# A hybrid decoder step on one core: linear attention's queries and keys decayed in place, and a planner that iterates with backward priorities

## The chip, the cores and the metric

The kernel runs on one core of one Trainium2 chip. The metric is the device time of one execution in microseconds (us), from the first to the last instruction and what lies around them. Five instruction streams run side by side: PE (TensorE, matmuls), DVE (VectorE), ACT (ScalarE), POOL (GpSimd) and SP (SyncE, which here issues all DMAs). Each works its own stream strictly in order.

## The reference

One decoder layer with two mixers side by side. For 2048 prompt rows and 64 sample rows (8 requests of 8 tokens):

```python
h = rmsnorm(x, norm_w)
q, k, v, qb, kb, vb, g_lr, gate_a, gate_b = split(h @ w_in)
o_a = attend(rope(rmsnorm(q)), rope(rmsnorm(k)), v)      # three dilated windows, 8 heads x 64
log_a = log_sigmoid(g_lr @ w_gate_up + b_gate) / 16       # one decay per token, head and key dim
o_b, s_fin = gla_chunked(qb / 8, kb, vb, log_a, s0)       # gated linear attention, 4 heads
y = x + concat(o_a * silu(gate_a), rmsnorm(o_b) * silu(gate_b)) @ w_out
```

Linear attention, for a chunk with `b = cumsum(log_a)`: the score of query t and key s ≤ t is the sum over key dims of `q[t] * k[s] * exp(b[t] - b[s])`; the output adds `q * exp(b)` times the state before the chunk; the new state is `exp(b_last) * state + (k * exp(b_last - b))^T v`. The outputs also hold the new keys and values and the states, for prompt and samples.

## The kernel before

All is float32 in and out. Projections and attention products run as pairs of f16 parts, linear attention in f32. The work has four stages, with the PE's projections woven through all of them:

1. Projections of v, q and k (`acc_v`, `acc_q`, `acc_k`; helper line L1614), row tiles of 128.
2. Dilated attention: scores `s` (L894) into PSUM, mask and maximum on DVE (L902), Exp on ACT (`p`, L905), transposes `t` on PE (L912), the split into f16 parts `pt` (ACT L874/L878, DVE L875, POOL L879), values `O` (L927). Beside it run the sample queries' scores against the key cache, called dots here: 104 loads of cached keys and 64 of queries, 128 products `pr` on POOL (L1469), each followed by a sum `sck` on DVE (L1470). The projections `acc_qkb`, then `acc_g` and `acc_vb`, fill PE.
3. Linear attention (`gla_core`, `gla_prompt`): the sample rows, then eight pieces `e` of 256 tokens, two chunks of 128 each. Seven levels B = 1, 2, 4 ... 64 build the scores within a chunk: at level B the queries of every second block of B tokens meet the keys of the block before. Each level needs scaled keys `ks` (L702), scaled queries laid out for two heads `qbd` (L706), matmuls `sc` (L730, L715) and a masked copy of the result (L736). The rest of `g`, `vb` and then `gb` projections fill PE; `so_gb` is the gate's SiLU on DVE (L1163, L1171), and `gw` its product on POOL (L1255).
4. Output: `combine` mixes the three attention branches and linear attention (`mix`), the mix is split and transposed (`mt`, `tm`), and `Y` (L1985) multiplies by `w_out`, whose f16 parts `w_o` are made by ACT L1144 and DVE L1145. The samples' attention over values (`OS`) fills in.

What sets the order: the program is traced, and then the class `Plan` writes one order for each of the five streams by hand. `depend` finds what must precede what, `price` gives each instruction a busy time and a latency, `rank` the longest path from each instruction to the end, `order` runs a list schedule with those ranks as priorities, and `fix` pins the result. So any change of a price or priority can move instructions anywhere in the program, within the dependences and the room in the buffers.

## Time and profile before

| | us |
|---|---|
| median of 3 runs (lowest to highest) | 1388.49 (1387.33 to 1389.8) |
| the profiled execution | 1387.66 |
| its span, first to last instruction | 1385.1 |
| PE busy | 1244.2 (90%) |
| DVE busy | 1008.1 (73%) |
| ACT busy | 844.7 (61%) |
| POOL busy | 639.5 (46%) |
| mean granted PE clock | 0.970 |

A row of the timeline gives the start, the duration, the engine, the source line, the operation, output<-inputs and a count; in square brackets stands how long the engine sat idle before and what ended that. A row of a table by stretches gives the stretch, its length, the busy time and instruction count of each engine it names (PE, PEld, DVE, ACT, POOL in this order), then the granted PE clock, the DMA engines' mean busy share and GB/s. In the groups, `x56 | 51.3, 921 | 11.9` reads: 56 instructions, 51.3 us busy, 921 ns each, 11.9 us idle before them. An f32 matmul is counted twice in the PE's rows (two records each).

### The profile page before, as it was taken

Reading aid. Unit: us, or ns where it says so; the run is one execution under the profiler, and the core shown is the slowest. Engines: PE = TensorE matmul, PEld = TensorE weight load, DVE = VectorE, ACT = ScalarE, POOL = GpSimd, SP = SyncE. Lnnn points to the kernel's source line nnn. Section 1 sums busy time; section 2 is a strip of 40 time slices with the busy share of each in tenths; the row PEclk is TensorE's granted clock in tenths of the full one; section 3 lists DMA queues with packets and bytes.
Section 4 is the critical chain, followed back from the end, with each engine's and each line's share of the span. In section 5 each row is a group of like instructions: output and inputs, shape, how many; then the busy total and the mean of one; then the engine's idle time right before and its main releaser. Section 6 shows DMA issues by size and latency. Waiting matters only on the chain.

```text
span 1385.1 us, 26375 instructions
## 1 busy us (share of the span) xinstructions
PE 1244.2 (90%) x8942; PEld 739.4 (53%) x8942; DVE 1008.1 (73%) x2459; ACT 844.7 (61%) x2259; POOL 639.5 (46%) x564
## 2 busy tenths in 40 slices
PE   5999988987889789998899999999989839999998
PEld 2444455555456556655667656665555415445443
DVE  6897787888889978767665338778889775566632
ACT  6465588786678869776778347787768541222220
POOL 0155447787677555543212546645574332233310
PEclk9999999998999999999999999999999969999999
DMA  8579747968986797899765534325334389999822
GB/s 298 179 194 268 206 132 202 226 199 213 207 288 178 170 308 242 248 249 280 187 181 154 144 102 110 109 84 179 103 100 145 104 309 344 343 380 345 323 79 70
DMA packets 236121, 283.25 MB, mean 205 GB/s; under 512 B 116353, under 2 KB 147154, under 8 KB 232914
## 3 DMA queue, kind: packets, MB, share of 16 engines
q1 hardware_dynamic: 235986, 281.57, 67.9%
q8 instruction: 70, 1.15, 0.4%
q14 instruction: 65, 0.53, 0.1%
HBM read 183.19 MB, written 75.24 MB: 187 GB/s over the span
## 4 chain that ended last, share of the span: by engine, by line
PE 36%; DVE 8%; ACT 7%; DMA 6%; issue 3%; POOL 1%; SPq 1%; DVEq 0%; ACTq 0%; POOLq 0%
PE Y L1985 10%; PE acc_vb L1614 4%; PE acc_g L1614 4%; PE acc_gb L1614 4%; DMA qb<-q_d 2%; PE OS L2234 1%; PE sc_e L730 1%; ACT p L905 1%; PE t L912 1%; PE O L1791 1%; PE acc_qkb L1614 1%; DMA o_d<-o 1%; DVE qbd L706 1%; PE O L1785 1%; PE O L927 1%
## 5 line engine op out<-in xcount | busy, mean ns | idle before, releaser
L1614 PEld LDWEIGHTS <-hr 128*128 128x128 f16 x1824 | 175.1, 99 | 125.0 <-issue 29.7
L1469 POOL TENSOR_TENSOR pr<-k,qb 128x512 f32<-128x512 f32 x128 | 176.9, 1382 | 133.4 <-DVE sck L1470 62.7
L905 ACT ACTIVATE p<-p,o 128x256 f32<-128x256 f32 (+1 forms) x384 | 172.7, 453 | 53.5 <-DVE o L902 43.7
L1614 PEld LDWEIGHTS <-hl 128*128 128x128 f16 x1248 | 119.7, 98 | 128.2 <-issue 18.7
L1985 PE MATMUL Y<-w_o,mh 128*128 128x512 f16 x768 | 181.1, 381 | 3.6 <-DVE xr L1992 1.7
L927 PE MATMUL O<-v,pt 128*128 128x128 f16 x1200 | 145.9, 224 | 8.6 <-POOL pt L879 3.5
L879 POOL TENSOR_TENSOR pt<-p,pt 128x512 f16<-128x512 f32 (+1 forms) x80 | 93.0, 1163 | 125.6 <-ACT pt L878 94.7
L912 PE MATMUL t<-ident,p 128*128 128x128 f32 x600 | 132.2, 294 | 16.3 <-ACT p L905 10.4
L1614 PE MATMUL acc_g<-w_g,hr 128*128 128x272 f16 (+1 forms) x768 | 130.6, 276 | 3.3 <-ACT vbs L1263 2.0
L1614 PE MATMUL acc_vb<-w_vb,hr 128*128 128x512 f16 x384 | 122.1, 384 | 1.6 <-DVE so_g L1163 1.5
L927 PEld LDWEIGHTS <-pt 128*128 128x128 f16 x1200 | 100.2, 101 | 43.3 <-POOL pt L879 7.2
L1470 DVE TENSOR_REDUCE sck<-pr 128x8 f32<-128x512 f32 x128 | 87.3, 682 | 48.9 <-POOL pr L1469 48.2
L1614 PE MATMUL acc_v<-w_v,hl 128*128 128x512 f16 x384 | 120.2, 384 | 2.0 <-DMA hl<-ht 1.0
L1614 PE MATMUL acc_k<-w_k,hl 128*128 128x512 f16 x384 | 114.8, 379 | 4.5 <-DVE vp L1276 2.9
L1614 PE MATMUL acc_q<-w_q,hl 128*128 128x512 f16 x384 | 116.2, 379 | 2.8 <-ACT zs_q L1189 2.4
L1985 PEld LDWEIGHTS <-mh 128*128 128x128 f16 x768 | 71.2, 98 | 84.5 <-issue 7.5
L894 PE MATMUL s<-kk,qq 128*128 128x256 f16 (+1 forms) x512 | 84.8, 270 | 29.4 <-DVE o L902 21.7
L912 PEld LDWEIGHTS t<-ident,p 128*128 128x128 f32 x600 | 79.3, 147 | 50.1 <-ACT p L905 28.0
L1614 PE MATMUL acc_gb<-w_gb,hr 128*128 128x512 f16 x384 | 95.7, 399 | 7.8 <-DVE so_gb L1163 7.8
L902 DVE CUSTOM_DVE_ANT_0 p<-s,m3w,scl_s 128x128 f32<-128x128 f32 (+1 forms) x256 | 87.8, 396 | 19.8 <-DMA o_d<-o 8.9
L2033 POOL TENSOR_TENSOR tc<-oc,w 128x512 f32<-128x512 f32 x32 | 42.8, 1354 | 118.7 <-DVE w L2025 67.9
L1614 PE MATMUL acc_qkb<-w_qkb,hr 128*128 128x512 f16 x288 | 85.1, 379 | 0.0
(534 smaller groups left out, 2723.1 us busy)
## 6 DMA issues: line engine op xcount, KB each, us to landing
k<-in_cache_k_win SPq DMA_DIRECT2D x104, 256.0 KB
sv_b<-in_cache_v_win SPq DMA_DIRECT2D x24, 1024.0 KB
hr<-h_d SPq DMA_DIRECT2D x44, 512.0 KB
qb<-q_d SPq DMA_DIRECT2D x64, 256.0 KB
oc<-o_d SPq DMA_DIRECT2D x48, 264.0 KB
o_d<-o SPq DMA_DIRECT2D x64, 132.0 KB
x<-in_x_prompt SPq DMA_DIRECT2D x16, 512.0 KB
h_d<-hl SPq DMA_DIRECT2D x16, 512.0 KB
```

The source lines that it names most:

```text
L706: DVE.tensor_tensor(qbd[:, :, :n].rearrange("p i (m B) -> p i m B", B=B), qv[:, :, 1, :].unsqueeze(1).to_broadcast([P, 2, M, B]), ev[:, 1: ...
L879: POOL.tensor_tensor(l, f, h, ALU.subtract)
L894: PE.matmul(s_ps[:, i * w : (i + 1) * w], q, k, start=(n == 0), stop=(n == len(prods) - 1),)
L902: DVE.tensor_tensor_reduce(s[:, sl], s_ps[:, sl], mask, neg, BIG, ALU.add, ALU.min, nmf(i))
L905: ACT.activation(s[:, sl], s[:, sl], AF.Exp, bias=nmf(i), scale=-1.0, accum_out=denf(i))
L912: PE.transpose(p_ps[:, i * P : (i + 1) * P], t["s"][:, i * P : (i + 1) * P], ident[:])
L927: PE.matmul(o_, t["pt"][:, c, (i * nb + b) * P : (i * nb + b + 1) * P], vf(i, b), start=(n == 0), stop=(n == 2 * nb - 1),)
L1469: POOL.tensor_tensor(pr[:], kt, qt, ALU.mult)
L1470: DVE.tensor_reduce(out, pr[:].rearrange("p (u k d) -> p u k d", u=2, k=4), AX.X, ALU.add)
L1614: PE.matmul(z, a_[:, k, :], w[:, p_, k, cols], start=(k == 0 and i == 0), stop=(k == KT - 1 and i == 2),)
L1985: PE.matmul(Y[:], a_[:, k, :], w_[:, part, k, :512], start=(i == 0), stop=(i == len(prods) - 1),)
L2033: eng.tensor_tensor(t_[:], oc[:, g, :, 0:64], w[:, g].unsqueeze(2).to_broadcast([P, NH, HD]), ALU.mult,)
```

## The change

**Linear attention.** Before, `b` is the running sum of the log decays (a scan on DVE, L673), and every level takes differences of `b` to the block's edge (two POOL subtractions `D`, L690 and L691), three Exps on ACT (`E`, L695) and two DVE multiplications into fresh buffers `ks` and `qbd`; all seven levels depend only on `b`. Now the decays themselves are used, `d = exp(log_a)`. Queries are multiplied by `d` once. At each level, two ACT copies spread the current queries into `qbd`, and the matmuls read the keys where they lie. After that, `decay()` multiplies in place: keys of even blocks by the odd neighbour's product (POOL), queries of odd blocks by the even neighbour's product (DVE), and a short DVE product pairs the block products up for the next level. After the last level the tile holds the queries decayed from the chunk's start and the keys decayed to its end, so the separate `qe` and `kd` work is gone. Each level now changes the tile that the next one reads. The buffer `kq` has three copies instead of two, `qbd` three, and `E`, `ks`, `D`, `b`, `eb` are gone. The matmuls are the same in number and shape.

```diff
@@ Plan.order
-                if not line or wide[0][0] <= line[0][0] + (bias if mode else -bias):
+                while recent and recent[0][0] < t - self.window:
+                    active -= recent.popleft()[1]
+                keep = mode and active > self.least * self.window
+                if not line or wide[0][0] <= line[0][0] + (bias if keep else -bias):
...
+                if int(s // self.window) > turn:
+                    half = work < 0.4 * self.window or int(s // self.window) > turn + 1
+                    turn, work = int(s // self.window), 0.0
...
+                own = self.busy[n] * (2 if half else 1)
@@ Plan, new
+    def settle(self, rounds, land, traffic, cross, bias, others=4):
...
+        others = [true.other(k) for k in range(others)]
+        self.lands = {n: x + land for n, x in self.lands.items()}
...
+        for _ in range(rounds):
+            out = self.order(prio, bias)[1]
+            prio = [-x for x in self.backward(self.start)]
+            end = sum(o.replay(out) for o in others)
+            if best is None or end < best[0]:
+                best = end, out
+        return best[1]
@@ gla_core
-        b = gt.tile([P, 2, n], F32, name=f"b_{tagp}", tag="bg", bufs=2)
-        for p in range(2):
-            DVE.tensor_tensor_scan(
-                b[:, p, :], scan_m[:, :n], la[:, p, :], 0.0, ALU.mult, ALU.add
-            )
-        eb = gt.tile([P, 2, n], F32, name=f"eb_{tagp}", tag="eb", bufs=2)
-        ACT.activation(eb[:], b[:], AF.Exp, scale=1.0 / 16.0)
+        ACT.activation(d[:], laf, AF.Exp, scale=1.0 / 16.0)
+        q, k = (f.rearrange("p a c -> p (a c)") for f in (qT, kT))
+        DVE.tensor_tensor(q, q, d[:], ALU.mult)
...
-            POOL.tensor_tensor(dv[:, 1], bv[:, :, 1, :], ref, ALU.subtract)
-            POOL.tensor_tensor(dv[:, 0], ref, bv[:, :, 0, :], ALU.subtract)
-            for i, (rows, half) in enumerate(
-                ((slice(0, P), 0), (slice(0, 64), 1), (slice(64, P), 1))
-            ):
-                ACT.activation(E[rows, i, :n], D[rows, half], AF.Exp, scale=1.0 / 16.0)
...
+            for i in range(2):
+                rows = slice(64 * i, 64 * i + 64)
+                ACT.activation(
+                    qbd[rows, i, :n].rearrange("p (m B) -> p m B", B=B),
+                    qv[rows, :, 1, :], AF.Copy,
+                )
+            part = whole.rearrange("p (m two) -> p m two", two=2)
+
+            def decay():
+                nonlocal whole, free
+                POOL.tensor_tensor(
+                    kv[:, :, 0, :], kv[:, :, 0, :], part[:, :, 1:2].to_broadcast([P, M, B]),
+                    ALU.mult,
+                )
+                DVE.tensor_tensor(
+                    qv[:, :, 1, :], qv[:, :, 1, :], part[:, :, 0:1].to_broadcast([P, M, B]),
+                    ALU.mult,
+                )
+                whole = sums[:, free : free + M]
+                free += M
+                DVE.tensor_tensor(whole, part[:, :, 0], part[:, :, 1], ALU.mult)
...
-        POOL.tensor_tensor(qe[:], qT, eb[:], ALU.mult)
@@ gla_decayed_keys
-        POOL.tensor_tensor(
-            kdf.rearrange("p (m s) -> p m s", s=seg),
-            bv[:, :, seg - 1 : seg].to_broadcast([P, m, seg]), bv, ALU.subtract,
-        )
-        ACT.activation(kd[:], kd[:], AF.Exp, scale=1.0 / 16.0)
-        POOL.tensor_tensor(kd[:], kd[:], kT, ALU.mult)
@@ end of tile_hymba
-    far = plan.rank()
-    plan.fix(plan.order([-f for f in far], 2000.0)[1])
+    plan.fix(plan.settle(8, 500.0, 1.1, 50.0, 1000.0))
```

**How it moves instructions.** The matmuls keep nearly their places: the projections and the order of the stages stay. Three places move.

POOL at the end of attention, before. `pr` is a dot, `pt` a split of attention; the name after `pr_` is the request and the token. These are the last of the 128 dots.

```order
L1469 TENSOR_TENSOR pr_7_6_8449<-k_7_6_8447,qb_6_8445 128x512
L879 TENSOR_TENSOR pt_4_1_8500<-p_4_1_8387,pt_4_1_8500 128x512
L1469 TENSOR_TENSOR pr_7_6_8452<-k_7_2_8324,qb_6_8445 128x512
L879 TENSOR_TENSOR pt_5_1_8619<-p_5_1_8505,pt_5_1_8619 128x512
L1469 TENSOR_TENSOR pr_7_3_8558<-k_7_3_8554,qb_3_8552 128x512
L1469 TENSOR_TENSOR pr_7_3_8561<-k_7_3_8556,qb_3_8552 128x512
L1469 TENSOR_TENSOR pr_7_7_8665<-k_7_7_8663,qb_7_8661 128x512
L879 TENSOR_TENSOR pt_6_1_8734<-p_6_1_8624,pt_6_1_8734 128x512
L1469 TENSOR_TENSOR pr_7_7_8668<-k_7_3_8556,qb_7_8661 128x512
```

POOL now, at the same dots. `kq_e` is the tile of keys and queries of a piece of linear attention.

```order
L1595 TENSOR_TENSOR pr_7_6_8449<-k_7_6_8447,qb_6_8445 128x512
L834 TENSOR_TENSOR kq_e_10021<-kq_e_10021,d_e_10050 128x256
L1595 TENSOR_TENSOR pr_7_6_8452<-k_7_2_8324,qb_6_8445 128x512
L834 TENSOR_TENSOR kq_e_10021<-kq_e_10021,sums_e_10053 128x128x2
L1595 TENSOR_TENSOR pr_7_3_8558<-k_7_3_8554,qb_3_8552 128x512
L834 TENSOR_TENSOR kq_e_10021<-kq_e_10021,sums_e_10053 128x64x4
L1595 TENSOR_TENSOR pr_7_3_8561<-k_7_3_8556,qb_3_8552 128x512
L834 TENSOR_TENSOR kq_e_10021<-kq_e_10021,sums_e_10053 128x32x8
```

The last dots stood among attention's splits, and now stand among the first piece's decays. Counted over the whole order of DVE: ahead of the 192nd of attention's 384 mask operations stood 80 sums of dots, now 36; ahead of the last mask stood all 128, now 98.

DVE within the last piece of linear attention, before and now. `Ac_e` is the masked copy of a level's scores, `so_gb` the gate.

```order
L736 COPY_PREDICATED Ac_e_13273<-gmask,sc_e_2_13335 128x128x2
L706 TENSOR_TENSOR qbd_9613<-kq_e_13275,E_9609 128x512
L702 TENSOR_TENSOR ks_9611<-kq_e_13275,E_9609 128x32x8
L706 TENSOR_TENSOR qbd_9605<-kq_e_13275,E_9601 128x512
L736 COPY_PREDICATED Ac_e_13273<-gmask,sc_e_4_13353 128x64x4
L702 TENSOR_TENSOR ks_9603<-kq_e_13275,E_9601 128x16x16
L1171 ISA so_gb_14079,gmax_b<-so_gb_14079,sa_gb_14081 128x512
```

```order
L873 COPY_PREDICATED Ac_e_13051<-gmask,sc_e_2_13103 128x128x2
L1297 ISA so_gb_13788,gmax_b<-so_gb_13788,sa_gb_13790 128x512
L1297 ISA gmax_b 128x1
L838 TENSOR_TENSOR kq_e_13053<-kq_e_13053,sums_e_13085 128x64x4
L844 TENSOR_TENSOR sums_e_13085<-sums_e_13085 128x64
L1271 SCALAR_TENSOR_TENSOR w_o_13591<-wr_o_6_13399,ns_o_13562,w_o_13591 128x512
L838 TENSOR_TENSOR kq_e_13053<-kq_e_13053,sums_e_13085 128x32x8
L873 COPY_PREDICATED Ac_e_13051<-gmask,sc_e_4_13118 128x64x4
```

A 512-wide and a 256-wide product for each level became one 256-wide product and a short one. On PE, between the scores of one level and those of the next level of the same piece stand 9.5 projection matmuls on average now (0 to 23; none in 3 of 48 places), 9.8 before (0 to 55; none in 20 of 48): the levels, which stood in bunches, are spread evenly. In the last four pieces it is 7.0 now.

DVE between linear attention and the output, before and now. `mn`, `w`, `dw` are combine's small tiles, `w_o` the second half of the output weights.

```order
L2015 TENSOR_TENSOR mn_14190<-oc_14179 128x8
L1145 SCALAR_TENSOR_TENSOR w_o_14248<-wr_o_0_14000,ns_o_14229,w_o_14248 128x512 x2
L1145 SCALAR_TENSOR_TENSOR w_o_14248<-wr_o_2_14003,ns_o_14229,w_o_14248 128x512 x2
L1145 SCALAR_TENSOR_TENSOR w_o_14248<-wr_o_4_14006,ns_o_14229,w_o_14248 128x512 x2
L1145 SCALAR_TENSOR_TENSOR w_o_14248<-wr_o_6_14009,ns_o_14229,w_o_14248 128x512 x2
L2016 TENSOR_TENSOR mn_14190<-mn_14190,oc_14179 128x8
```

```order
L2135 TENSOR_TENSOR w_13941<-oc_13929,mn_13940 128x24
L1271 SCALAR_TENSOR_TENSOR w_o_13998<-wr_o_0_13750,ns_o_13979,w_o_13998 128x512 x2
L2139 TENSOR_TENSOR dw_13942<-w_13941,oc_13929 128x24
L1271 SCALAR_TENSOR_TENSOR w_o_13998<-wr_o_2_13753,ns_o_13979,w_o_13998 128x512
L2140 TENSOR_TENSOR mn_13940<-dw_13942 128x8
L1271 SCALAR_TENSOR_TENSOR w_o_13998<-wr_o_2_13753,ns_o_13979,w_o_13998 128x512
L2141 TENSOR_TENSOR mn_13940<-mn_13940,dw_13942 128x8
```

The first tile's combine stood behind all eight weight tiles, and is now interleaved with them. After the last matmul of linear attention PE still has 47 projection matmuls before and 50 now, and then nothing until `tm`.

## The prediction

> **What bounds the kernel now.** I read the page's engine shares first, then the table by stretches, then PE's waits within the two stretches that lose most.

> ```profile
> PE 1244.2 (90%) x8942; PEld 739.4 (53%) x8942; DVE 1008.1 (73%) x2459; ACT 844.7 (61%) x2259; POOL 639.5 (46%) x564
> ```

> ```profile
> 170.00:540.00 370.00, 317.09 (x2359) 208.56 (x2357) 318.52 (x809) 281.52 (x821) 243.40 (x185) 0.97 0.80 212
> 540.00:680.00 140.00, 126.36 (x980) 82.82 (x980) 100.68 (x318) 104.02 (x329) 65.62 (x51) 0.98 0.90 245
> 680.00:745.00 65.00, 64.24 (x575) 46.16 (x573) 39.25 (x173) 53.87 (x193) 8.25 (x7) 1.00 0.69 184
> 745.00:930.00 185.00, 181.44 (x1444) 120.87 (x1442) 112.59 (x247) 113.37 (x304) 98.55 (x117) 1.00 0.39 114
> 930.00:1104.00 174.00, 158.04 (x1136) 91.64 (x1135) 143.21 (x282) 125.69 (x313) 93.56 (x94) 0.92 0.39 123
> 1104.00:1140.00 36.00, 13.33 (x72) 6.96 (x71) 29.46 (x76) 15.18 (x31) 16.07 (x15) 0.70 0.83 280
> 1140.00:1385.00 245.00, 235.80 (x1683) 114.27 (x1681) 131.81 (x285) 55.38 (x86) 58.60 (x45) 0.99 0.73 271
> ```

> PE is the bound, and its work stays the same, so only what PE loses can be won: idle time, and matmuls at a low clock. Idle (length less PE busy) is 52.9 us in attention's first part (170 to 540), 13.6 and 0.8 in the rest of it, 3.6 in the first half of linear attention, 16.0 in its second half, 22.7 in the passage to the output, 9.2 in the output. Where PE loses, DVE is nearly full: 318.5 of 370 us (86%) and 143.2 of 174 (82%). Who is waited for there:

> ```profile
> ACT p L905 <- DVE o L902: 37.2, 27, 4.1
> PEld t L912 <- ACT p L905: 23.8, 51, 3.1
> PE s L894 <- DVE o L902: 22.4, 25, 2.8
> ```

> ```profile
> PE acc_gb L1614 <- DVE so_gb L1163: 7.8, 3, 4.2
> PE sc_e L730 <- DVE ks L702: 3.4, 2, 2.2
> ```

> The first three are of 170 to 680, the last two of 930 to 1104. All lead to DVE: attention's masks come late, and in linear attention the gate (which frees a PSUM buffer) and the keys. A wait costs more than itself:

> ```profile
> 1081.75 2.29 PE L1614 MATMUL acc_gb<-w_gb,hr 128*128 128x512 f16 x5 [3.16 <-DVE so_gb L1163]
> 1083.97 1.12 PE L730 MATMUL sc_e<-qbd,ks 128*64 128x64 f32 x16
> 1085.03 2.74 PE L1614 MATMUL acc_gb<-w_gb,hr 128*128 128x512 f16 x6
> 1089.42 2.75 PE L1614 MATMUL acc_gb<-w_gb,hr 128*128 128x512 f16 x12
> 1080.00:1085.00 5.00, 3.25 (x21) 1.50 (x20) 4.99 (x12) 3.28 (x8) 1.83 (x2) 0.60 0.51 161
> ```

> After 3.16 us idle, 6 matmuls take 2.74 us, where 12 take 2.75 shortly after; the granted clock is 0.60. So each such stall is paid about twice. Between 930 and 1104 the clock of 0.92 is worth up to 0.08 x 174 = 13.9 us beside the 16.0 idle: 29.9 in all.

> [...]

> **The change, part by part.** (a) Linear attention's own work, for the eight prompt pieces:

> ```profile
> L706 DVE TENSOR_TENSOR qbd<-kq_e,E 128x512 f32<-128x512 f32 x56 | 51.3, 921 | 11.9 <-ACT E L695 7.2 <-PE sc_e L730 4.6
> L702 DVE TENSOR_TENSOR ks<-kq_e,E 128x256 f32<-128x256 f32 x56 | 39.6, 715 | 7.7 <-ACT E L695 5.3 <-PE sc_e L715 2.0 <-PE sc_e L730 0.4
> L673 DVE TENSOR_TENSOR_SCAN b_e<-scan_m,la_e 128x256 f32<-128x256 f32 x16 | 11.0, 726 | 0.1
> L706 DVE TENSOR_TENSOR qbd<-kq_smp,E 128x128 f32<-128x128 f32 x3 | 1.0, 348 | 0.3 <-POOL D_smp L691 0.2
> L690 POOL TENSOR_TENSOR D_e<-b_e 128x256 f32<-128x256 f32 x56 | 46.0, 821 | 53.1 <-DVE b_e L673 25.1 <-ACT E L695 19.1 <-PE O_s L1844 3.8
> L691 POOL TENSOR_TENSOR D_e<-b_e 128x256 f32<-128x256 f32 x56 | 41.2, 735 | 0.0
> L765 POOL TENSOR_TENSOR kd_e<-kd_e,kq_e 128x512 f32<-128x512 f32 x8 | 11.3, 1416 | 1.3 <-ACT kd_e L764 1.3
> L744 POOL TENSOR_TENSOR qe_e<-kq_e,eb_e 128x512 f32<-128x512 f32 x8 | 11.0, 1373 | 0.0
> L760 POOL TENSOR_TENSOR kd_e<-b_e 128x512 f32<-128x512 f32 x8 | 9.8, 1227 | 0.0
> L695 ACT ACTIVATE E<-D_e 64x256 f32<-64x256 f32 x112 | 45.7, 408 | 1.0
> L695 ACT ACTIVATE E<-D_e 128x256 f32<-128x256 f32 x56 | 23.1, 412 | 11.1 <-POOL D_e L691 4.6 <-DVE ks L702 3.6 <-DVE ra_o_smp L612 2.5
> ```

> DVE loses 51.3 + 39.6 + 11.0 = 101.9 us. It gains 56 query products at 715 ns (40.0), 8 products with d at 921 (7.4), and 56 sums: 8 at 715 and 48 shorter ones at no more than 348 (22.4). Net -32 us. POOL loses 46.0 + 41.2 + 11.3 + 11.0 + 9.8 = 119.3 and gains 56 key products at about 778 ns (43.6): -76. ACT loses 68.8 of Exps and gains 112 copies at 408 ns (45.7): -23. None of this is on PE; it pays only where PE waited for DVE. The relief is 32/8 = 4 us of DVE for each piece; with five of the eight in the second half, its 143.2 us fall to some 123 of 174, 71%. That should remove most of the 16.0 idle us and the slow matmuls behind them, but each level is now a chain:

> ```profile
> 863.58 0.63 POOL L690 TENSOR_TENSOR D_e<-b_e 128x256 f32<-128x256 f32 x1 [0.16 <-ACT E L695]
> 864.17 1.06 POOL L691 TENSOR_TENSOR D_e<-b_e 128x256 f32<-128x256 f32 x1
> 865.72 0.69 PE L730 MATMUL sc_e<-qbd,ks 128*64 128x64 f32 x16
> 869.20 1.15 PE L730 MATMUL sc_e<-qbd,ks 128*64 128x64 f32 x32
> ```

> Scores (0.69), the keys' decay on POOL (0.63 to 1.06), the next scores: 1.3 to 1.8 us a level. The other branch, two ACT copies (0.82) and the queries' decay (0.72), is 1.5. To fill this PE has 7.0 projection matmuls on average in the last four pieces, at 2.75/12 = 0.23 us: 1.6 us; in the first four it has 12.0, some of them half as wide. So the chain is covered, with little over. I take 13 of the 29.9 us. [...]

> [...]

> (b) The dots:

> ```profile
> L1469 POOL TENSOR_TENSOR pr<-k,qb 128x512 f32<-128x512 f32 x128 | 176.9, 1382 | 133.4 <-DVE sck L1470 62.7
> L1470 DVE TENSOR_REDUCE sck<-pr 128x8 f32<-128x512 f32 x128 | 87.3, 682 | 48.9 <-POOL pr L1469 48.2
> ```

> Ahead of the middle of attention stand 44 fewer (36, not 80): 44 x 0.682 = 30.0 us of DVE and 60.8 of POOL leave the stretch where PE loses 52.9. The second half takes 62 instead of 48: +9.5 us of DVE, where DVE is at 72% and PE idles 13.6. The last 30, 20.5 us of DVE and 41.5 of POOL, go to the start of linear attention, where DVE is busy 112.6 of 185 us and POOL gets 76 us back. Their loads of keys and queries move along, from a DMA share of 0.80 to 0.90 to one of 0.39. If PE won all of the 30.0 us, it would be 30; the waits are a chain through DVE, ACT and PE, and only DVE gets lighter, so I take 23 of it, less 3 for the second half: 20. Bounds: -14 (no gain in the first part, and the second loses as much again as the 13.6 + 0.8 it idles now) and +45 (all but 8 of the 52.9).

> (c) The passage to the output. PE runs out of projections and waits for the first mix:

> ```profile
> 1120.17 6.40 DVE L1145 SCALAR_TENSOR_TENSOR w_o<-wr_o,ns_o,w_o 128x512 f16<-128x512 f32 x8 [0.37 <-ACT w_o L1144]
> 1134.01 0.69 DVE L2040 TENSOR_TENSOR mix<-tc,gal 128x512 f32<-128x512 f32 x1 [1.22 <-POOL tc L2039]
> 1135.85 0.82 PE L1950 MATMUL tm<-ident,mt 128*128 128x128 f16 x6 [19.26 <-ACT mt L1940]
> ```

> Before, combine's first tile stands behind 6.40 us of weight splitting; now its small operations run between the splits. The splits still come first for the most part and the loads land no earlier, so I take 3, between 0 and 6. That linear attention ends earlier does not shorten the passage: 50 projection matmuls cover it, before 47.

> (d) PE changes between f32 products and the rest 230 times, 196 before. From the two rows of `sc`, 16 records cost 0.69 and 32 cost 1.15, so a start costs at most 0.23; 34 x 0.23 = 8 at most, 0 at least, and I take 2, since most of it is the last matmul's drain.

> Sum: 20 + 13 + 3 - 2 = 34 us off the profiled execution's 1387.7, which is 0.8 under the median of 1388.5. So 1354 us. The start, 745 to 930 and the output keep PE full and should not move.

> **Rivals.** Attention gains nothing: its waits are latency through mask, Exp and transpose, not DVE's queue. For it: DVE is 86% busy, not 100%. Against it: of the waits quoted, 37.2 and 22.4 us end at DVE itself. Then 1388.5 - 14 = 1374.

> Both stages come out nearly full, because the planner now counts the slow clock too: 45 + 25 + 6 - 2 = 74 off, 1315. For it speaks that a stall is paid twice now; against it that attention's chain remains.

> [...]

> No change that can be measured: the new order loses in attention (keys' loads later, other prices) the 14 us of (b)'s lower bound, which are what it wins elsewhere: 1388.5 - 14 + 14, the time before.

> **How the numbers follow.** Chances: my forecast 0.50 (own range 1333 to 1368), attention without gain 0.17, both full 0.12, the levels' chain 0.10, no change 0.11. A difference under 0.2% (2.8 us) can't be told from none. Faster: the first three and a third of the last, 0.83; same 0.05; slower 0.12. The range 1322 to 1388 takes in the forecast, the first rival, half of the second and of the last.

> **What would show it.** Right: PE idle between 170 and 540 falls to about 35 us, with fewer DVE-ended waits of `s` and `t`; in the second half of linear attention PE idles under 8 us at a clock of 0.96 or more; the gap before `tm` is 16 to 19 us; the output takes 245 us. Wrong: waits of `sc` or its weights for POOL `kq_e` of over 10 us in all (the chain), attention ending later than 745 with PE idle as before, or POOL dots that hold up the first piece's decays.

## The result, and the profile after

The changed kernel takes **1325.7 us** (1319.1 to 1328.2, four runs) beside 1389.1 of the kernel before, measured beside it: ratio 0.953, interval 0.948 to 0.958. The forecast was 1354, with an own range of 1333 to 1368 and an outer one of 1322 to 1388: the change gained 63 us, nearly twice the 34 of the sum. Of the profiled execution's 1327.4 us the span is 1325.4, which is 59.7 less than before.

The page's engine shares, after:

```profile
PE 1241.1 (94%) x8942; PEld 733.6 (55%) x8942; DVE 954.0 (72%) x2450; ACT 820.2 (62%) x2191; POOL 545.7 (41%) x475
```

PE does the same matmuls in 3.1 us less, and idles 84.3 us, not 140.9. Both kernels are now cut at the same events: the first and the last transpose `t` of attention, the end of the last matmul that reads linear attention's state (`Sbd`), the first `tm`. Between the second and third the stretch is halved. The table by stretches, before and then after:

```profile
0.00:171.60 171.60, 149.51 (x720) 69.09 (x721) 134.14 (x274) 95.72 (x187) 56.93 (x55) 1.00 0.77 231
171.60:750.60 579.00, 511.69 (x3948) 340.61 (x3947) 459.88 (x1315) 444.91 (x1361) 316.91 (x243) 0.97 0.81 216
750.60:926.75 176.15, 172.59 (x1363) 114.50 (x1362) 107.68 (x227) 104.69 (x278) 95.78 (x113) 1.00 0.40 117
926.75:1102.90 176.15, 160.19 (x1167) 93.21 (x1164) 145.17 (x285) 128.37 (x319) 94.76 (x96) 0.92 0.38 121
1102.90:1135.90 33.00, 11.45 (x58) 5.56 (x57) 25.41 (x71) 14.34 (x29) 13.09 (x13) 0.74 0.80 262
1135.90:1385.10 249.20, 238.79 (x1702) 116.40 (x1702) 135.86 (x290) 56.73 (x88) 62.01 (x47) 0.99 0.73 273
```

```profile
0.00:159.00 159.00, 135.88 (x658) 63.07 (x659) 127.09 (x258) 88.44 (x172) 48.45 (x51) 0.99 0.76 225
159.00:717.30 558.30, 527.53 (x4112) 353.09 (x4111) 442.89 (x1309) 451.00 (x1389) 280.68 (x219) 0.98 0.81 218
717.30:880.60 163.30, 158.93 (x1182) 99.45 (x1181) 107.38 (x228) 83.54 (x211) 90.72 (x92) 1.00 0.59 167
880.60:1043.90 163.30, 161.67 (x1225) 94.04 (x1224) 118.93 (x298) 124.05 (x306) 53.29 (x59) 1.00 0.41 137
1043.90:1076.80 32.90, 15.62 (x77) 7.52 (x75) 22.40 (x64) 14.52 (x30) 10.60 (x8) 0.77 0.61 213
1076.80:1325.40 248.60, 241.52 (x1702) 116.42 (x1702) 135.35 (x298) 58.61 (x89) 61.97 (x47) 0.98 0.76 277
```

Length less PE busy: attention loses 36.5 us of idle time (67.3 to 30.8), the second half of linear attention 14.4 (16.0 to 1.6, its clock from 0.92 to 1.00), the passage 4.3, the output 3.3; the start gains 1.0 and the first half 0.8. PE's waits, after:

```profile
PE tm L2068 <- ACT mt L2058: 17.3, 1, 17.3
PE s L1020 <- DVE o L1028: 6.5, 9, 1.9
PE t L1038 <- ACT p L1031: 3.9, 8, 1.2
```

Attention's waits for the mask fell from 22.4 to 6.5 us. The dots now reach into linear attention: 100 products of the 128 start in attention's stretch. The groups of the dots over the whole program, and within attention, after:

```profile
L1596 DVE TENSOR_REDUCE sck<-pr 128x8 f32<-128x512 f32 x128 | 87.2, 681 | 50.9 <-POOL pr L1595 50.4
L1595 POOL TENSOR_TENSOR pr<-k,qb 128x512 f32<-128x512 f32 x100 | 131.6, 1316 | 154.2 <-DVE sck L1596 68.6 <-DMA k<-in_cache_k_win 34.8 <-issue 32.2
L1596 DVE TENSOR_REDUCE sck<-pr 128x8 f32<-128x512 f32 x99 | 67.4, 681 | 30.7 <-POOL pr L1595 30.3
```

The last column matters. A sum that stands at the head of DVE's queue while POOL still multiplies can hold up the masks behind it. Before, all dots lay in attention, so the group quoted in the prediction gives 87.3 us busy and 48.9 idle, 136.2 together; now it is 67.4 + 30.7 = 98.1. Not all of this counts. Matched in order with their score matmuls, the 384 masks show that before at most 65 of the 87.3 us busy and 30 of the 48.9 idle fell while a mask that had not begun had its scores finished; now it is 44 and 17.

### The profile page after: what moved, and what is told of

Its sections match the earlier page's. It is cut to its first block, busy times and chain, and to the rows that moved or that the text cites. A ratio compares the mean times of both kernels' runs of the same rounds, so it can differ in the third digit from the quotient of the medians.

```text
span 1325.4 us, 26186 instructions
## 1 busy us (share of the span) xinstructions
PE 1241.1 (94%) x8942; PEld 733.6 (55%) x8942; DVE 954.0 (72%) x2450; ACT 820.2 (62%) x2191; POOL 545.7 (41%) x475
## 3 DMA queue, kind: packets, MB, share of 16 engines
q8 instruction: 70, 1.15, 0.4%
## 4 chain that ended last, share of the span: by engine, by line
PE 52%; DVE 13%; ACT 11%; DMA 8%; issue 8%; POOL 5%; SPq 1%; DVEq 0%; POOLq 0%; ACTq 0%
PE Y L2103 11%; PE acc_gb L1740 5%; PE acc_k L1740 4%; ACT p L1031 4%; PE acc_vb L1740 3%; POOL pr L1595 3%; PE acc_q L1740 3%; PE t L1038 2%; PE acc_qkb L1740 2%; PE sc_e L867 2%; PE acc_v L1740 2%; PE OS L2352 2%; PE acc_g L1740 2%; PE O L1053 2%; PE s L1020 2%
## 5 line engine op out<-in xcount | busy, mean ns | idle before, releaser
L1595 POOL TENSOR_TENSOR pr<-k,qb 128x512 f32<-128x512 f32 x128 | 167.8, 1311 | 176.9 <-DVE sck L1596 79.7
L1740 PEld LDWEIGHTS <-hl 128*128 128x128 f16 x1248 | 120.2, 98 | 131.2 <-issue 15.9
L1053 PE MATMUL O<-v,pt 128*128 128x128 f16 x1200 | 149.1, 221 | 6.5 <-POOL pt L1005 2.8
L1740 PE MATMUL acc_g<-w_g,hr 128*128 128x256 f16 (+1 forms) x768 | 124.1, 279 | 2.7 <-ACT vbs L1389 2.4
L1740 PE MATMUL acc_vb<-w_vb,hr 128*128 128x512 f16 x384 | 111.9, 385 | 5.3 <-DVE so_g L1289 4.9
L1740 PE MATMUL acc_q<-w_q,hl 128*128 128x512 f16 x384 | 110.9, 379 | 1.3 <-DVE vp L1402 0.8
L1038 PEld LDWEIGHTS t<-ident,p 128*128 128x128 f32 x600 | 78.1, 144 | 34.7 <-ACT p L1031 19.6
```

The source lines that it names most:

```text
L1038: PE.transpose(p_ps[:, i * P : (i + 1) * P], t["s"][:, i * P : (i + 1) * P], ident[:])
L1053: PE.matmul(o_, t["pt"][:, c, (i * nb + b) * P : (i * nb + b + 1) * P], vf(i, b), start=(n == 0), stop=(n == 2 * nb - 1),)
L1595: POOL.tensor_tensor(pr[:], kt, qt, ALU.mult)
L1740: PE.matmul(z, a_[:, k, :], w[:, p_, k, cols], start=(k == 0 and i == 0), stop=(k == KT - 1 and i == 2),)
```

## The experiments

PE's idle time (us) by the same events in every profiled execution; "dots" are the sums of dots ahead of the 192nd and the last of the 384 masks. Times are medians; the kernel before had 1389.1 beside the change, 1385.7 beside 1 to 4, 1388.8 beside 5 to 8 and 1389.1 beside 9 to 12, and each ratio is to its own. The idle times are those of one execution, which in 4, 7, 8, 10 and 12 lay 3 to 9 us from the median.

| kernel | dots | time, ratio to before (interval) | start | attention | linear attention, halves | passage | output | PE busy |
|---|---|---|---|---|---|---|---|---|
| before | 80, 128 | 1389.1 | 22.1 | 67.3 | 3.6, 16.0 | 21.6 | 10.4 | 1244.2 |
| the change | 36, 98 | 1325.7, 0.953 (0.948 to 0.958) | 23.1 | 30.8 | 4.4, 1.6 | 17.3 | 7.1 | 1241.1 |
| 1 new linear attention, old planner | 31, 94 | 1337.0, 0.966 (0.962 to 0.969) | 29.4 | 38.8 | 5.0, 2.2 | 8.9 | 14.2 | 1236.4 |
| 2 old linear attention, new planner | 46, 121 | 1334.1, 0.963 (0.960 to 0.965) | 22.7 | 35.5 | 2.6, 8.3 | 18.8 | 9.1 | 1234.2 |
| 3 the change, dots early | 66, 128 | 1340.1, 0.967 (0.964 to 0.970) | 24.2 | 44.4 | 1.7, 2.4 | 16.5 | 6.8 | 1240.4 |
| 4 before, dots late | 36, 99 | 1404.6, 1.013 (1.009 to 1.017) | 24.1 | 47.1 | 17.3, 27.0 | 21.5 | 10.4 | 1258.8 |
| 5 as 1, dots early | 84, 128 | 1383.4, 0.995 (0.992 to 0.997) | 32.9 | 67.0 | 3.6, 1.9 | 8.9 | 14.1 | 1253.1 |
| 6 the change, one round | 37, 98 | 1343.6, 0.968 (0.966 to 0.970) | 28.1 | 30.0 | 3.3, 0.8 | 18.6 | 10.3 | 1250.2 |
| 7 the change, old prices | 27, 82 | 1319.6, 0.951 (0.948 to 0.954) | 18.9 | 38.8 | 6.4, 0.9 | 19.1 | 6.2 | 1231.2 |
| 8 as 2, one round | 78, 128 | 1373.7, 0.991 (0.988 to 0.994) | 27.3 | 41.8 | 6.3, 17.8 | 19.3 | 10.9 | 1257.7 |
| 9 the change, no slow-clock model | 28, 90 | 1322.8, 0.952 (0.951 to 0.954) | 23.6 | 31.9 | 4.7, 1.6 | 17.3 | 8.9 | 1232.9 |
| 10 before, slow-clock model alone | 80, 128 | 1375.2, 0.990 (0.989 to 0.992) | 22.6 | 60.3 | 2.6, 9.1 | 18.7 | 10.0 | 1245.9 |
| 11 the change, longer levels | 31, 77 | 1323.5, 0.953 (0.950 to 0.957) | 24.2 | 35.4 | 1.8, 2.5 | 16.5 | 8.5 | 1233.8 |
| 12 as 7, no slow-clock model | 29, 92 | 1333.3, 0.960 (0.957 to 0.964) | 20.3 | 39.5 | 7.8, 1.7 | 16.8 | 7.6 | 1233.6 |

**Each half alone (1, 2), and the dots alone (3, 4).** Theory A is the prediction's: late dots and the lighter levels do it, whichever planner places them. Theory B: the planner does attention's part.

```diff
-    plan.fix(plan.settle(8, 500.0, 1.1, 50.0, 1000.0))          # 1: on the change,
+    far = plan.rank()                                           # and no slow-clock model
+    plan.fix(plan.order([-f for f in far], 2000.0)[1])
```

> The new linear attention, ordered by the planner of before (ranks as priorities, one pass, bias 2000, no slow clock in the model). Its order already has the dots late: 31 sums of dots ahead of the 192nd mask and 94 ahead of the last (before: 80 and 128; the change: 36 and 98). Theory A, the late dots relieve attention and the lighter linear attention does the rest, whatever the planner: most of the gain is here, about 45 of the 63 us, so some 1344 us, with PE idle in attention near 40 us. Theory B, the planner's own work (slow clock, backward pass, altered prices) brings attention's part: only linear attention's 14 us and the passage's 4 are here, some 1370 us, with PE idle in attention near 65 us.

Kernel 2 is the kernel before with the whole new `Plan` and the last line of the change.

> The linear attention of before, ordered by the new planner. The dots come only partly late: 46 ahead of the 192nd mask, 121 ahead of the last. Theory A: about half of attention's relief and nothing in linear attention, some 1370 us. Theory B: attention gains its whole 36 us, linear attention little, some 1350 us.

```diff
-            out = self.order(prio, bias)[1]                     # 3: on the change
+            early = [x - 600000.0 * d for x, d in zip(prio, mine)] + prio[len(mine):]
+            out = self.order(early, bias)[1]                    # d is 1 for a dot's instructions
```

> The changed kernel, with the dots (their loads, products and sums) preferred in each forward pass by 600 us of priority, so that 66 stand ahead of the 192nd mask and all 128 ahead of the last, nearly as before. Theory A: attention loses about 20 to 25 us of its gain, some 1348 us. Theory B: no more than 5 us, since linear attention gets the room that the dots leave: some 1328 us.

```diff
-    plan.fix(plan.order([-f for f in far], 2000.0)[1])          # 4: on the kernel before
+    late = [150000.0 * d for d in plan.dots()] + [0.0] * len(far)
+    plan.fix(plan.order([x - f for x, f in zip(late, far)], 2000.0)[1])
```

> The kernel before, with its own planner, and the dots put back by 150 us of priority, so that 36 stand ahead of the 192nd mask and 99 ahead of the last, as in the change. Theory A: attention gains 20 to 30 us and the old linear attention, which now holds 29 dots too, loses up to 10: some 1368 us. Theory B: no gain, 1385 to 1395 us.

Neither theory held. A came near in 1 (1344 us and an idle time near 40 forecast, 1337.0 and 38.8 measured), 3 fell between the two, and 2 and 4 lay outside of both. Each half alone gives most of the gain, 3.4% and 3.7% of 4.7%, so they largely replace each other; yet late dots alone made the kernel slower by 1.3%. Attention and the two halves of linear attention in kernel 4:

```profile
174.40:729.90 555.50, 508.38 (x3949) 338.95 (x3948) 439.63 (x1287) 441.93 (x1360) 275.82 (x216) 0.98 0.79 209
729.90:926.35 196.45, 179.18 (x1290) 114.04 (x1287) 116.07 (x224) 94.26 (x244) 117.97 (x127) 0.94 0.50 146
926.35:1122.80 196.45, 169.43 (x1231) 101.50 (x1232) 160.59 (x316) 141.80 (x352) 107.35 (x111) 0.90 0.34 112
```

With the same number of matmuls (3949 records, 3948 before) attention idles 20.2 us less and is 23.5 shorter. That is the prediction's 20, measured with no other edit, and the masks' share of PE's waits in attention falls from 22.4 us to 6.8:

```profile
PE s L901 <- DVE o L909: 6.8, 9, 1.5
```

The dots' loads and POOL's products move along with the sums, and none of these runs separates the three; the wait for attention's own loads (`kk`), 7.1 us before, is 3.2 here. But linear attention takes 392.9 us, not 352.3. The dots within it, in kernel 4 and in kernel 1, whose levels are the new ones:

```profile
L1477 DVE TENSOR_REDUCE sck<-pr 128x8 f32<-128x512 f32 x28 | 19.1, 683 | 27.8 <-POOL pr L1476 27.7
```

```profile
L1596 DVE TENSOR_REDUCE sck<-pr 128x8 f32<-128x512 f32 x33 | 22.4, 678 | 15.8 <-POOL pr L1595 15.7
```

PE's waits in kernel 4 that kernel 1 does not have (`ra_o_c` belongs to the norm of linear attention's output):

```profile
PE sc_e L737 <- DVE ra_o_c L620: 4.8, 1, 4.8
PE sc_e L737 <- DVE ks L709: 4.8, 5, 1.2
PE sc_e L737 <- DVE qbd L713: 4.7, 2, 3.6
```

Among the old levels 28 sums hold DVE for 46.9 us, and among the new levels 33 sums hold it for 38.2, while kernel 1 idles 7.2 us in the whole stretch. But PE does not stand behind the sums. In kernel 4 the last of them ends at 809.0, 79 us into linear attention, and until then PE is busy with projections for the most part. The levels' first score matmul starts 110.9 us into the stretch, where it was 78.0 before and is 85.1 in kernel 1, in which sums stand among the levels until 850.5. The idle time comes afterwards. Between 160 and 240 us into the stretch PE has 59 records of projections beside 208 of scores in kernel 4, and had 206 beside 232 before; kernel 4, then before:

```profile
889.90:969.90 80.00, 58.52 (x404) 38.63 (x405) 57.78 (x115) 47.30 (x123) 38.49 (x44) 0.77 0.26 84
910.60:990.60 80.00, 76.39 (x570) 46.32 (x568) 63.69 (x133) 61.63 (x156) 40.64 (x48) 0.94 0.41 129
```

Here lie 21.5 of the 44.3 us that kernel 4 idles in linear attention, at a clock of 0.77; before it was 3.6 us at 0.94. So in this order the dots stood ahead of the levels, the levels began later, and the projections that used to cover them had been spent. Whether the old linear attention would bear the dots among its levels, as the new one does in kernel 1, was not tried: kernel 4 is one order, and POOL's load, DVE's and the order were not separated by a run.

**The dots' place under the new levels (5), and what the planner's parts do (6 to 8).** Theory C: attention's idle time follows the dots' place. Theory D: the backward priorities win attention's other 16 us. Theory E: the altered prices carry it.

```diff
-    plan.fix(plan.settle(8, 500.0, 1.1, 50.0, 1000.0))
+    plan.fix(plan.settle(1, 500.0, 1.1, 50.0, 1000.0))          # 6; 8 is the same on kernel 2
```

> The changed kernel with one round of the planner instead of eight: forward ranks only, no backward priorities, but the altered prices and the slow-clock model stay. Ahead of the 192nd mask stand 37 sums of dots (36 in the change). Theory C, the dots' place sets attention's idle time (20 us fewer idle in attention when they alone were moved): PE idles about 31 us in attention and 5 in linear attention as in the change, 1326 us, at most 1331. Theory D, the backward priorities win attention's other 16 us: attention idles 39 to 47 us and the time is 1335 to 1345.

```diff
-    plan.fix(plan.settle(8, 500.0, 1.1, 50.0, 1000.0))
+    plan.fix(plan.settle(8, 0.0, 1.0, 35.0, 1000.0))            # 7
```

> The changed kernel with eight rounds, but with the unaltered prices (loads not 500 ns later, DMA factor 1.0, 35 ns between engines). 27 dots ahead of the 192nd mask. Theory C: as the change, 1326 us, at most 1331. Theory E, the pessimistic prices carry the gain because loads and hand-overs then are ordered with slack: attention idles 40 us or more and the time is 1335 to 1345. Theory D says 1326 too.

```diff
-    plan.fix(plan.order([-f for f in far], 2000.0)[1])          # 5: on kernel 1
+    early = [-200000.0 * d for d in plan.dots()] + [0.0] * len(far)
+    plan.fix(plan.order([x - f for x, f in zip(early, far)], 2000.0)[1])
```

> New linear attention with the old planner, and the dots preferred by 200 us, which puts 84 of them ahead of the 192nd mask and all 128 ahead of the last (80 and 128 in the kernel before; 31 and 94 without the preference, 1337.0 us). Theory C: attention idles 28 us more, 67 as before, linear attention stays at 7, so 1337 + 28 = 1365 us. Theory D: the dots are a smaller part, some 14 us as in the change with early dots (44.4 against 30.8 idle), so 1351 us or less.

Kernel 8:

> Old linear attention, new planner with one round: altered prices and slow-clock model, forward ranks only. 78 dots ahead of the 192nd mask, all 128 ahead of the last, as in the kernel before. Theory C: attention idles 60 to 67 us and linear attention 11 to 20, so 1334 + 28 = 1362 us or more. Theory D, the same number by another cause: without backward priorities 1355 to 1375. If the prices and the slow-clock model alone do it, the time stays at 1334 to 1340 with the dots early, and both theories fall.

Kernel 5 is the clearest of all. Attention in kernel 1 and in kernel 5, each with its wait for the masks, which came back in 5:

```profile
153.20:720.30 567.10, 528.33 (x4080) 348.85 (x4079) 447.90 (x1306) 453.12 (x1389) 285.52 (x218) 0.99 0.78 212
PE s L1020 <- DVE o L1028: 4.6, 7, 1.4
```

```profile
158.70:768.70 610.00, 543.04 (x4077) 352.17 (x4076) 485.14 (x1339) 457.08 (x1389) 330.54 (x250) 0.97 0.78 213
PE s L1027 <- DVE o L1035: 20.1, 20, 4.4
```

Nothing but the dots' priority was edited, though the planner moves other instructions with them, and PE has nearly the same work in this stretch (4080 and 4077 records). Attention idles 67.0 us again, 28.2 more, and its matmuls take 14.7 us longer at a clock of 0.97 instead of 0.99: 42.9 us of the 46.6 by which the spans differ. So with the old planner the dots' place is all of attention's gain in idle time, and it is worth twice what I priced. C was right on the idle time and 18 us low on the time.

C fails where the new planner places early dots. In 8, with 78 dots ahead of the middle, attention idles 41.8 us, not 60 to 67, and in 3, with 66, it idles 44.4. The time of 8 is still 1373.7; in its profiled execution, which was 9.1 us slower, linear attention idles 24.1 and PE is busy 13.5 us longer than before. Eight rounds instead of one are worth 2.9% of the time before on the old linear attention (8 against 2, with the dots moved back from 78 to 46) and 1.5% on the new (6 against the change). D gave the time of 6, but not by its cause: attention idles 30.0 us there, as in the change; of the 15.9 us in span 6.8 are idle, in the start and the output above all, and 9.1 are PE busy. Old prices (7) lose nothing, so E falls; 7 and the change can't be told apart by their intervals.

**The slow-clock model (9, 10, 12) and the levels' chain (11).** Theory F: the clock model only trims. Theory G: it keeps PE from stalling in attention.

```diff
-                keep = mode and active > self.least * self.window
+                keep = mode                                     # 9, and 12 on kernel 7
...
-                own = self.busy[n] * (2 if half else 1)
+                own = self.busy[n]
```

> The changed kernel without the slow-clock model in the planner (both parts of it), the rest of the planner as in the change. 28 dots ahead of the 192nd mask. Theory F, attention idles little because the dots come late, and the clock model only trims: idle in attention 30 to 36 us, 1326 to 1334 us. Theory G, the clock model is what keeps PE from stalling in attention (with it and the other prices, old linear attention idled 41.8 us there at early dots, 67.3 without): attention idles 45 us or more, 1340 us or more.

Kernel 10 is the reverse: the kernel before with these two edits of the change and nothing else.

> The kernel before with the slow-clock model in its planner and nothing else: old linear attention, forward ranks, old prices, old bias. 80 dots ahead of the 192nd mask, as before. Theory F: as the kernel before, 1385 to 1392 us, attention idles 60 to 68. Theory G: attention idles about 42 us as with one round of the whole new planner, and the time is 1374 us or less.

Kernel 12:

> The changed kernel with the unaltered prices and without the slow-clock model: what is left of the new planner is backward priorities and eight rounds judged by replays. 29 dots ahead of the 192nd mask. Theory F: 1318 to 1328 us, attention idles 31 to 39 us as with the plain prices alone (1319.6 us, 38.8 idle). Theory G: 1335 us or more.

G falls: without the model the change keeps its time (9), and with it alone attention idles 60.3 us (10). But on the old kernel it wins 14 us, which F did not expect. Of the 15.9 us of span that it wins in the profiled execution, 10.0 lie in linear attention, whose second half before had a clock of 0.92 and idled 16.0 us; attention is 3.2 shorter and idles 7.0 less. The second half now:

```profile
917.45:1088.60 171.15, 162.07 (x1208) 95.18 (x1206) 142.35 (x294) 134.54 (x336) 95.08 (x99) 0.96 0.41 128
```

With the old prices it is worth 14 us again (12 against 7; 12 fell between the numbers of F and G), with the altered ones nothing. The six plans with the new linear attention and late dots (the change, 1, 6, 7, 9, 12) lie between 1319.6 and 1343.6: such a spread comes from the order alone, and I have no single cause for it.

```diff
             def decay():
+                POOL.tensor_tensor(                             # 11: keys times ones
+                    kv[:, :, 0, :], kv[:, :, 0, :], ones[:].unsqueeze(2).to_broadcast([P, M, B]),
+                    ALU.mult,
+                )
```

> The changed kernel with each key decay of a level preceded by a multiplication of the same keys by ones on POOL, so that each of the 56 levels has one more POOL operation of about 0.7 us in its chain (39 us of POOL in all); the output stays the same. My theory, the levels are covered by projections and POOL has room: PE idles at most 6 us more in linear attention, 1326 to 1333 us. [...]

The added operations, and both halves of linear attention in 11:

```profile
L834 POOL TENSOR_TENSOR kq_e<-kq_e,ones 128x256 f32<-128x256 f32 x56 | 38.7, 692 | 47.5 <-PE sc_e L871 34.1 <-PE sc_e L855 10.6 <-DVE ra_o_c L754 2.7
689.80:864.55 174.75, 172.92 (x1331) 111.61 (x1329) 126.55 (x259) 94.85 (x237) 129.22 (x133) 1.00 0.68 199
864.55:1039.30 174.75, 172.24 (x1298) 102.91 (x1296) 124.40 (x306) 127.06 (x311) 82.69 (x98) 0.99 0.45 144
```

A POOL operation of 0.69 us more in each of the 56 levels costs no time that shows: PE idles 4.3 us here, 6.0 in the change. The chain has that much cover, though the planner had also moved more dots behind it; what more than 0.69 us a level would cost was not tried. POOL is busy 211.9 of 349.5 us here, 61%, more than the 57% of kernel 4, so POOL's load alone does not make PE idle there.

## Why the prediction was right or wrong

**Linear attention: right in kind, and priced low if anything.** 13 of 29.9 us were forecast, for idle time and slow matmuls together. The idle time alone fell by 13.6 in both halves, and the clock of the second half rose to 1.00, which the prediction had priced at up to 13.9 more. Kernel 5 shows the same with the dots as early as before (19.6 to 5.5 us of idle time), though there the start idles 10.8 us more and PE is busy 8.9 longer, so that only 0.5% is left. The engines' relief was near: DVE gained 56.8 us of new work where 69.8 were priced, POOL 40.2 for 43.6. DVE was cheaper mostly because the level products took 544 ns on average, where the `ks` row by which they were priced has 715; after:

```profile
L838 DVE TENSOR_TENSOR kq_e<-kq_e,sums_e 128x256 f32<-128x256 f32 x48 | 26.1, 544 | 15.8 <-ACT qbd L826 15.5
L834 POOL TENSOR_TENSOR kq_e<-kq_e,sums_e 128x256 f32<-128x256 f32 x48 | 33.2, 691 | 89.5 <-PE sc_e L867 50.3 <-issue 17.7 <-PE sc_e L851 9.9
```

POOL waits for PE's scores far more than PE for POOL: the weight loads of `sc` wait 2.9 us in all for POOL's `kq_e`, where over 10 was the sign of the chain. So the levels' chain, which had a chance of 0.10, did not bound linear attention, and 11 shows that there was room to spare.

**Attention: the mis-sized term.** The step said that only DVE gets lighter, and took 20 of the 30.0 us that the sums occupy it. The idle time fell by 36.5. In the first two thirds of the stretch (up to 550 before, 537 now) it fell from 54.4 to 20.1, where the prediction looked for about 35 of 52.9 to be left between 170 and 540. Moving the dots alone does win 20.2 (4). Three things were left out. First, a sum holds DVE longer than its 0.682 us: the row quoted in the prediction showed 48.9 us of DVE idle for POOL's products beside 87.3 busy, and I counted only the latter; at most 30 of the 48.9 stood in a mask's way. Second, the lost time was priced as idle time alone, though the prediction had shown slow matmuls behind a stall (after 3.16 us idle 6 took 2.74 us, where 12 took 2.75 shortly after): in 5 against 1 there were 14.7 us of slower matmuls to 28.2 idle. Third, the planner has a share of its own, which I put at nothing: with the old linear attention it cuts attention's idle time to 35.5 with 46 dots ahead of the middle (2), and to 41.8 with 78 (8). The steps from 4 (47.1) to 1 (38.8) and to the change (30.8) are 8.3 and 8.0 us. Those are differences between whole plans: 1 also has 132 more matmul records inside attention than before, and I can't say how much of the 8.3 is due to that.

**What I had as independent was not.** The sum treats the dots' move as won by itself. Kernel 4 shows that it costs 1.3% with the old levels, and kernel 5 that the new levels without it win only 0.5%. Together they win 3.4% (1): with the new linear attention the dots found room there. Whether that is because it is lighter, or because of where the planner put the dots in each, is not shown. The sum came out with the right sign since the change does both; that part was luck.

**Passage, mode changes, and the rest.** The wait before `tm` is 17.3 us, in the 16 to 19 forecast; the passage gains 4.3 for 3. The output was to keep its time and gained 0.6 in length. The 2 us for more changes between f32 products and the rest were put low because most of the 0.23 us of a start was taken for the last matmul's drain. Before, in the 24 places where other products follow the scores of L730 without a pause at full clock, the first of them starts 0.154 to 0.155 us after the last score, where scores start (1.15 - 0.69) / 16 = 0.029 apart: 0.125 of the 0.23 lies there. The 2 us itself is an estimate that no run shows alone, and it was too low if the changes are the cause of this: counted record by record, each from the end of the one before, the levels' scores take 45.2 us of PE, 39.3 before, with the same matmuls. In the records of the clock, PE was busy 56.3 us at half speed before and 27.7 now, which is worth 14.3 us; PE busy fell by only 3.1. The scores are 5.9 of the 11.2 between, and the rest stays open.

**The rivals.** "Nothing in attention" and "no change" are refuted by the table. "Both stages nearly full" is what the change comes nearest to: linear attention is full, attention halfway. The cause that I gave it, the slow-clock model, is refuted by 9.

## What to carry to other kernels

A helper's work that stood in line on an engine held up ready work here by its busy time and by waiting for its own input: of the sums' 87.3 us busy and 48.9 idle at most 65 and 30 us fell while a mask had its scores finished. So read both columns of its group, and ask how much of them falls while other work is ready. Before moving it, look at what it pushes back in the receiving stage, and at what is left to cover that; late dots won 2.9% of the time in one program and lost 1.3% in another. And once a hand-written planner sets the order, price a change in it by whole plans: six orders with late dots differ by 24 us here with the same instructions.

## What the runs showed of the hardware

Over these 14 profiles PE is busy between 1231.2 and 1258.8 us with the same matmuls; by least squares each us of idle time goes with 0.33 us of slower matmuls (correlation 0.74). So over whole programs an us of idle time came with 1.3 us of span, where the prediction read two from one stall. That is a correlation: the profiles differ in more than their idle time.

In the trace of the change some of the level products on DVE last longer where a POOL operation runs beside them, and end a fixed time after it. All 48 (shortest, median and longest in ns, then two of them in the timeline with POOL beside them):

```profile
L838 DVE TENSOR_TENSOR kq_e<-kq_e,sums_e x48: 413/426/1548, 805.6 to 1020.7; 128x256 f32<-128x256 f32 x48
```

```profile
861.58 0.74 POOL L834 TENSOR_TENSOR kq_e<-kq_e,sums_e 128x256 f32<-128x256 f32 x1 [1.64 <-PE sc_e L867]
861.91 0.68 DVE L838 TENSOR_TENSOR kq_e<-kq_e,sums_e 128x256 f32<-128x256 f32 x1
862.27 1.23 POOL L775 TENSOR_TENSOR Ac_e<-ident,dd_e 128x512 f32<-128x512 f32 x1
894.60 1.04 POOL L775 TENSOR_TENSOR Ac_e<-ident,dd_e 128x512 f32<-128x512 f32 x1 [2.00 <-ACT full L883]
894.85 1.07 DVE L838 TENSOR_TENSOR kq_e<-kq_e,sums_e 128x256 f32<-128x256 f32 x1
895.60 0.93 POOL L834 TENSOR_TENSOR kq_e<-kq_e,sums_e 128x256 f32<-128x256 f32 x1
```

In the last three rows POOL's first operation ends at 895.64 and DVE's product at 895.92. The 24 products that no POOL operation overlaps all take 0.41 to 0.46 us, while of the 24 overlapped ones 11 take 0.50 to 1.55; each of these 11 ends 0.28 to 0.29 us after a POOL operation that had begun before it. For the other 13 POOL began later, or ended within 0.15 us of the product's start, or was a memset. The price for DVE is small here: mean less median is 544 - 426 = 118 ns for each level product, 6 us over 48, since 37 of the 48 were not lengthened.
